# Loop order of transfers: two stores, then two loads, per pair of tiles, in an instance normalisation bound by its transfers

## Chip, cores, metric

One core of a Trainium2 chip. The metric is device time in microseconds (us), median of the executions of a run. Every run names its state; all those compared here were recorded as fast.

## The reference

```python
x: (256, 256, 4096) float32, standard normal;  eps = 1e-5
mean = np.mean(x, axis=2, keepdims=True)
var = np.var(x, axis=2, keepdims=True)
return ((x - mean) / np.sqrt(var + eps)).astype(np.float32)
```

65,536 rows of 4096 numbers are normalised one by one: 1 GiB is read and 1 GiB written.

## The kernel before

A tile is 512 rows (128 partitions x 4 rows, 8 MiB); there are 128 tiles and three buffers. The issuing queue (SyncE) starts all transfers; VectorE and ScalarE compute. VectorE's first pass takes the row sums and multiplies the tile by 1/4096 in place ("in-place means"), which the later scale undoes; ScalarE takes the sums of squares; both share the last pass. The parts that matter here:

```python
BUFS = 3; L0 = 2; rounds = (ntiles - 5) // BUFS          # 41
def store(s, t):
    take(S, done[s], K + 1)                              # wait for the compute of this tile
    S.dma_start(out=rows_of(out_t, t), in_=X[s][:, :, :]).then_inc(stored[s], 16)
def load(s, t, wait=True):
    if wait:
        take(S, stored[s], 16)                           # wait until the buffer's last store has landed
    S.dma_start(out=X[s][:, :, :], in_=rows_of(x_t, t)).then_inc(loaded[s], 16)
# VectorE, per tile (cut)
take(V, loaded[s], 16)
for r in range(4):
    V.tensor_scalar(out=x[:, r, :], in0=x[:, r, :], scalar1=1.0 / d, ..., accum_out=mean[s][:, r:r+1]).then_inc(means, 1)
...   # reciprocal, bias, then four passes x*rstd+nbias, each .then_inc(done[s], 1)
# issuing queue (cut): tile 0 in halves, then
with S.Fori(0, rounds) as i:
    for t in range(L0, L0 + BUFS):
        store(t % BUFS, (t, BUFS, rounds, i))
        load((t + 2) % BUFS, (t + 2, BUFS, rounds, i))
```

## Time and profile before

| | before |
|---|---|
| median, range | 4962.77 us, 4962.52 to 4963.97 (3 runs) |
| span of the profiled run | 4960.0 us |
| VectorE / ScalarE busy | 66% / 49% |
| DMA engines busy, rate | 100% of the span, 433 GB/s |

The prediction shows the lines that carry this.

The issuing queue in order of time (start, duration of the issue, line, what):

```profile
1003.20 0.34 SPq L165 DMA_DIRECT2D out_dram<-x  x1
1003.78 0.35 SPq L170 DMA_DIRECT2D x<-in_x_dram  x1
1042.14 0.34 SPq L165 DMA_DIRECT2D out_dram<-x  x1
1042.72 0.35 SPq L170 DMA_DIRECT2D x<-in_x_dram  x1
```

A store and the load two tiles ahead go out together, every 38.9 us here.

### The profile page before, as it was taken

How to read it: one execution, taken by the hardware profiler on the slowest of the kernel's cores; microseconds unless marked ns; L12 is line 12 of the kernel's file. 1: busy time of each engine (PE TensorE's matmuls, PEld its weight loads, DVE VectorE, ACT ScalarE, POOL GpSimd, SP SyncE). 2: the span in 40 equal slices, each digit the busy share in tenths (PEclk: the TensorE clock that was granted, in tenths of full speed). 3: DMA queues.
4: the chain of work that ended last, by engine and by line, in shares of the span. 5: the costliest groups of instructions: out<-in, count | busy, mean ns of one | idle time of the engine just before them, and what ended most of it. 6: DMA issues, size and time to landing. Idle time of an engine off the chain costs nothing.

```text
span 4960.0 us, 5954 instructions
## 1 busy us (share of the span) xinstructions
DVE 3298.0 (66%) x2049; ACT 2407.6 (49%) x1412; POOL 0.2 (0%) x4
## 2 busy tenths in 40 slices
DVE  6666666666666666666666666666666666666666
ACT  4454444554445544455445544455444554445544
POOL 0000000000000000000000000000000000000000
DMA  9999999999999999999999999999999999999999
GB/s 423 431 437 432 431 437 432 432 438 433 434 435 432 435 434 432 436 434 432 436 434 432 437 433 432 438 433 432 438 432 434 435 433 435 434 432 436 434 432 403
DMA packets 37298, 2147.52 MB, mean 433 GB/s; under 512 B 4144, under 2 KB 4144, under 8 KB 4144
## 3 DMA queue, kind: packets, MB, share of 16 engines
q1 hardware_dynamic: 37296, 2147.50, 100.0%
q14 instruction: 2, 0.02, 0.0%
HBM read 1073.74 MB, written 1073.74 MB: 433 GB/s over the span
## 4 chain that ended last, share of the span: by engine, by line
DVE 62%; another core or an unknown queue 31%; issue 4%; DMA 2%; ACT 0%; DVEq 0%; ACTq 0%; SPq 0%
DVE x L87 44%; DVE x L112 17%; DMA x<-in_x_dram 1%; DVE nbias L100 1%; DMA out_dram<-x 1%; DVE rstd L98 1%; ACT junk L137 0%; DVEq L68 0%; DVEq L225 0%; ACT L146 0%; ACT std L146 0%; DVEq L193 0%; ACTq L68 0%; ACTq L67 0%
## 5 line engine op out<-in xcount | busy, mean ns | idle before, releaser
L87 DVE TENSOR_SCALAR_CACHE_REDUCE x<-x 128x4096 f32<-128x4096 f32 x512 | 2232.3, 4416 | 1579.9 <-DMA x<-in_x_dram 1579.9
L137 ACT ACTIVATE junk<-x,mean 128x4096 f32<-128x4096 f32 x512 | 1883.1, 3678 | 2366.7 <-DVE x L87 2366.7
L112 DVE TENSOR_SCALAR x<-x,rstd,nbias 128x4096 f32<-128x4096 f32 (+1 forms) x512 | 1004.2, 2004 | 33.9 <-DVE nbias L100 29.3
L151 ACT ACTIVATE x<-x,nbias,rstd 128x3072 f32<-128x3072 f32 x130 | 383.2, 2948 | 146.2 <-DVEq L68 146.2
L137 ACT ACTIVATION_READ_ACCUMULATOR junk<-x,mean 128x1 f32 x512 | 95.5, 186 | 0.0
L146 ACT ACTIVATE std<-ss,eps_tile 128x2 f32<-128x2 f32 x256 | 75.6, 295 | 19.1
L98 DVE RECIPROCAL rstd<-std 128x2 f32<-128x2 f32 x256 | 40.7, 159 | 19.4 <-ACT std L146 19.4
L100 DVE SCALAR_TENSOR_TENSOR nbias<-mean,rstd 128x2 f32<-128x2 f32 x256 | 41.1, 161 | 8.9
L87 DVE DVE_READ_ACCUMULATOR x<-x 128x1 f32 x512 | 42.4, 83 | 0.0
L137 ACT ACT_TABLE_LOAD x1 | 1.3, 1283 | 1.2 <-DVE eps_tile L222 1.2
L146 ACT ACT_TABLE_LOAD x1 | 1.3, 1283 | 0.1
L222 DVE MEMSET eps_tile<- 128x1 f32 x1 | 0.1, 59 | 1.0 <-SPq L192 1.0
L259 POOL MEMSET const-bfloat16-1.0<- 128x1 bf16 x1 | 0.1, 103 | 0.0
L259 POOL MEMSET const-uint8-127<- 128x1 uint8 x1 | 0.1, 101 | 0.0
L259 POOL MEMSET const-float32-0.0<- 128x1 f32 x1 | 0.1, 99 | 0.2 <-issue 0.2
L259 POOL MEMSET const-float32-1.0<- 128x1 f32 x1 | 0.1, 98 | 0.0
## 6 DMA issues: line engine op xcount, KB each, us to landing
out_dram<-x SPq DMA_DIRECT2D x4, 4096.0 KB, 19.4
x<-in_x_dram SPq DMA_DIRECT2D x2, 4096.0 KB, 16.8
x<-in_x_dram SPq DMA_DIRECT2D x127, 50.3
out_dram<-x SPq DMA_DIRECT2D x126, 31.5
```

The source lines that it names most:

```text
L87: V.tensor_scalar(out=x[:, r, :], in0=x[:, r, :], scalar1=1.0 / d, scalar2=None, op0=ALU.mult, op1=ALU.add, accum_out=mean[s][:, r : r + 1 ...
L98: mine(V.reciprocal(out=rstd[s][:, c], in_=std[s][:, c]))
L100: mine(V.scalar_tensor_tensor(out=nbias[s][:, c], in0=mean[s][:, c], scalar=-1.0 / d, in1=rstd[s][:, c], op0=ALU.mult, op1=ALU.mult))
L112: V.tensor_scalar(out=x[:, r, f], in0=x[:, r, f], scalar1=rstd[s][:, c], scalar2=nbias[s][:, c], op0=ALU.mult, op1=ALU.add,).then_inc(dn, 1)
L137: mine(A.activation(out=junk, in_=x[:, r, :], func=AF.Square, bias=mean[s][:, c], scale=-float(d), accum_out=ss[s][:, c]))
L146: A.activation(out=std[s][:, c], in_=ss[s][:, c], func=AF.Sqrt, bias=eps_tile, scale=1.0 / d**3).then_inc(stds, 1)
L151: A.activation(out=x[:, last, :Q], in_=x[:, last, :Q], func=AF.Identity, bias=nbias[s][:, c], scale=rstd[s][:, c]).then_inc(dn, 1)
L222: V.memset(eps_tile, eps / d**2).then_inc(ready, 1)
L259: nc = _bacc.Bacc("TRN2", target_bir_lowering=False, num_devices=1)
```

## The change

The intent: halve the number of changes between reading and writing HBM, by sending two stores, then two loads. A load now goes into the buffer of a store that was issued just before it.

```diff
                 load(1, 1, wait=False)
+                load(2, 2, wait=False)
                 store_half(0, 0, 0)
                 store_half(0, 0, 1)
-                load(2, 2, wait=False)
                 store(1, 1)
                 take(S, stored[BUFS], 16)
                 load(0, 3)
-                with S.Fori(0, rounds) as i:
-                    for t in range(L0, L0 + BUFS):
-                        store(t % BUFS, (t, BUFS, rounds, i))
-                        load((t + 2) % BUFS, (t + 2, BUFS, rounds, i))
-                load(last % BUFS, last)
-                store((last - 2) % BUFS, last - 2)
-                store((last - 1) % BUFS, last - 1)
+                load(1, 4)
+                with S.Fori(0, 20) as i:
+                    for j in range(L0, L0 + 6, 2):
+                        for t in (j, j + 1):
+                            store(t % BUFS, (t, 6, 20, i))
+                        for t in (j + 3, j + 4):
+                            load(t % BUFS, (t, 6, 20, i))
+                for op, t in ((store, 122), (store, 123), (load, 125), (store, 124), (load, 126), (load, 127),
+                              (store, 125), (store, 126)):
+                    op(t % BUFS, t)
```

The two orders are called the old order and the pair order below. A "turn" is the place where the loads end and stores begin. The "ring" is the row of transfers that have been issued and not yet carried out; it "runs dry" when the DMA engines have nothing left to do. "Stretch", in the expectations, means packets that take longer than usual.

## The prediction

> **What bounds the kernel now.** I read the page from the top: first who is busy, then whether the transfers ever pause, then what the issuing queue waits for, and last how much work lies ahead of a transfer when it is issued. The first view is the page's busy shares with its transfer lines.
>
> ```profile
> DVE 3298.0 (66%) x2049; ACT 2407.6 (49%) x1412; POOL 0.2 (0%) x4
> ...
> DMA  9999999999999999999999999999999999999999
> ...
> DMA packets 37298, 2147.52 MB, mean 433 GB/s; under 512 B 4144, under 2 KB 4144, under 8 KB 4144
> ...
> HBM read 1073.74 MB, written 1073.74 MB: 433 GB/s over the span
> ```
>
> VectorE is idle for a third of the span and ScalarE for half; the 16 DMA engines are full in all 40 slices. The bytes are the least possible (1 GiB in, 1 GiB out), so 2147.5 MB at 433 GB/s is the whole 4960 us. The next view puts stretches of equal length side by side; the columns are the busy time of each engine, granted clock, DMA share and GB/s.
>
> ```profile
> 464.40:851.40 387.00, 257.89 (x160) 187.43 (x110) 0.00 (x0) 1.00 1.00 433
> 851.40:1238.40 387.00, 257.87 (x160) 187.45 (x110) 0.00 (x0) 1.00 1.00 434
> 2000.00:2387.00 387.00, 258.52 (x161) 188.06 (x111) 0.00 (x0) 1.00 1.00 434
> 4400.00:4787.00 387.00, 257.68 (x161) 187.45 (x110) 0.00 (x0) 1.00 1.00 434
> ```
>
> Ten tile periods of 38.7 us each fill such a stretch; the DMA share is 1.00 in every one. Nothing in the steady state waits for compute. Taking the packet records of the trace one by one gives the floor: nearly all (30,880 of 32,384) of the 64 KB packets took 2418 ns, loads and stores alike. One tile transfer is 8 such packets per DMA engine plus a 4-byte semaphore packet of 9 ns, some 19.35 us, and two of them are the 38.7 us period.
>
> Third, the waits of the issuing queue (who waited for whom, total us, times, longest), and the issues (KB each where stated, median us from issue to landing):
>
> ```profile
> SPq L68 <- DVE x L112: 4756.7, 130, 38.6
> SPq L68 <- DMA out_dram<-x: 47.7, 3, 30.7
> ...
> x<-in_x_dram SPq DMA_DIRECT2D x127, 50.3
> out_dram<-x SPq DMA_DIRECT2D x126, 31.5
> ```
>
> The issuer nearly always waits for VectorE to finish a tile, which looks like a compute bound and isn't one. A store lands 31.5 us after its issue, though it takes only 19.35: it stands 12.1 us behind work that is already queued. Those 12 us are the margin of the present order. A load, issued half a microsecond later, lands at 50.3, that is 12 + 2 x 19.3.
>
> [...]
>
> **The change, part by part.** It moves only issues and their waits on the issuing queue; the instruction listings of VectorE and ScalarE are the same but for line numbers, and so are count, size and shape of the 259 transfers.
>
> (a) Bytes: unchanged. The floor stays: per DMA engine 253 whole tile transfers x 19.35 us + 6 half ones x 9.7 = 4954 us. (The quickest spacing that the semaphore packets show is 19.319 us, as successive packets overlap a little: 4946.) To this come 2.0 us to the first packet and 1.8 us after the last (4958.2 of 4960.0).
>
> (b) Changes of direction: from about 256 to about 130. What is one worth? The packets longer than 2418 ns tell. Their excess sums to 3.5 us per DMA engine on average over the whole run, of which 1.1 us is at the first load-to-store boundary (near 39 us, packets of 3.4 to 4.0 us). The rest stands at the ends of loads that a store follows, and fades out by about 550 us; then boundary after boundary costs nothing. The engines begin in step (their semaphore packets lie 0.6 us apart in the first transfers) and are pulled apart at these boundaries: the spread is 3.3 us at the 12th transfer, 6.1 at the 48th, then 6.31 constantly up to the 204th, 8.2 near the end. So the last engine ends some 6.4 us after most others (4958.2 against 4951.8). My reading is that they get in each other's way only where many turn at once. The end is set by the slowest engine, so at the very best the change saves about 6 us (0.13%). If half the turns meant half the drift it would save 3; if the drift goes on until the engines are spread, which I find likelier since it levels off by itself, it saves almost nothing and only takes twice as long to get there. I take 1 us.
>
> (c) New waits. Let T be the landing of the first load of a pair, tile j+1. The ring then holds load j+2 (to T+19.4), store j (to 38.7), and after these come store j+1 (to 58.1), load j+3 (to 77.4), load j+4 (to 96.8). Compute takes 26.3 us a tile (from the timeline: 1015.7, first mean, to 1042.1, store issue). Store j+1 can be issued at T+26.4 and is needed at T+38.7: margin 12.3 us, what it was. Load j+3 goes into the buffer of store j, so it waits for that store to land, T+40 or so, and is needed at T+58.1: margin 17 or so. Load j+4 waits for store j+1, T+59.5, needed at T+77.4: 18. Store j+2, computed from T+26.3 to T+52.3, issued at T+60, needed at T+96.8: 37. No link is negative, so the ring never runs dry and the new direct wait of a load for the store just before costs nothing.
>
> (d) Head. Loading tile 2 ahead of the stores of tile 0 lets the ring hold work until about 60 us (2 + 3 x 19.35); the stores of tile 0 end at about 80. Store 1 is issued where before it was, at 74.5: the tightest place, some 5 us of margin. No gain either, since the ring was never dry in the head before.
>
> (e) Tail. Load 127 lands at the same distance from the end: stores 125, 126 and the two halves of 127 follow it as before. The last issue was at 4941.2, 7.3 us ahead of its turn on the slowest engine. Unchanged: 0.
>
> Sum: 4962.8 + 0 (a) - 1 (b) + 0 (c, d, e) = 4961.8.
>
> **Rivals.** *The turn of direction is costly and the change saves much.* For it: packets at the first turns are up to 1.6 us longer. Against: from about 1000 to 4000 us no packet is more than 0.3 us over, with a turn each 19.35 us; at most 6 us in all are to be had: 4956. *Two stores in a row overrun something on the way to HBM.* For it: late stores (from the 214th transfer) are 0.06 us longer on the slowest engine. Against: stores 125, 126, 127 already follow each other without a load, and come at 19.40 and 19.41 us where 19.35 is usual. At 0.06 us for each of 63 pairs, 4 us more: 4966. *The load's wait for the store just ahead makes the ring run dry.* If landing took over 15 us longer than I take it to, each pair would lose the difference; a 1 us hole in each of 63 pairs makes 5025. The margins in (c) speak against it.
>
> **Range and chances.** 4961.8, with 4957 (most of the drift saved) to 4967 (drift or late store stretch grows). Two per cent are 99 us, or 1.6 us in each of 63 pairs; nothing within reach of the order is that big on the fast side, and on the slow side only a hole in the ring that I have overlooked. Faster 0.005, same 0.98, slower 0.015.
>
> **What would show it.** DMA share 1.00 and 434 GB/s in the same stretches. VectorE's busy time stays at 3298 and its total wait for loads near 1580 us, but in some 65 waits of about 25 us in place of 126 of 12.6. Of the issuer's waits some 2000 us pass from VectorE to the stores' landing (per pair 13 + 19 = 32 us, x 62), leaving about 2750. Loads land in about 37 us after issue. The prediction is wrong if a steady stretch shows a share under 0.99, or if packets after 1000 us are not 2418 ns; step (b) is wrong if the last engine ends within 3 us of the others.

What the trace does show is the rate: 65536 B / 2418 ns = 27.1 GB/s per DMA engine, 434 for 16, with 30,880 of 32,384 packets at those 2418 ns while VectorE was busy for 66% of the span. That a changed order of issues is only a changed order of transfers, and costs nothing as long as the ring never runs dry, was the assumption; part (c) rests on it, and on margins worked out from the trace. The landings fit it (31.5 us after its issue for a store, 50.3 for the load behind it), and so do the two orders without compute, timed later (e5 4960.6 us, e6 4961.5).

## More of the kernel before

The page's rate in 40 slices of 124 us, in GB/s:

```profile
GB/s 423 431 437 432 431 437 432 432 438 433 434 435 432 435 434 432 436 434 432 436 434 432 437 433 432 438 433 432 438 432 434 435 433 435 434 432 436 434 432 403
```

The slices differ because a packet is counted whole in the slice where it starts (16 packets of 64 KB more or less are some 8 GB/s); there is no hole: between 600 and 4900 us the packet records never show fewer than 16 packets under way.

## The result

The changed kernel took 4975.77 us (median of 4 runs, 4972.83 to 4979.39) against 4962.65 (4 runs, 4961.47 to 4963.97): ratio 1.0027, 95% interval 1.0012 to 1.0041. It is 13 us slower, within 2% as forecast, but outside the stated range of 4957 to 4967. Ratios are the mean time of one kernel's fast runs over that of the other's of the same rounds, so not quite the ratio of the medians.

The views of the changed kernel that answer to those of before: the page's rate lines,

```profile
DMA  9999999999999999999999999999999999999999
GB/s 422 437 430 436 431 436 431 435 432 436 431 433 433 434 434 430 432 435 431 435 430 432 431 433 434 432 432 434 433 431 436 431 431 434 434 432 435 431 431 399
```

the same stretches (busy time of VectorE and ScalarE, clock, DMA share, GB/s),

```profile
464.40:851.40 387.00, 256.53 (x161) 186.53 (x111) 0.00 (x0) 1.00 1.00 433
851.40:1238.40 387.00, 256.00 (x159) 187.42 (x110) 0.00 (x0) 1.00 1.00 434
2000.00:2387.00 387.00, 257.00 (x161) 186.99 (x111) 0.00 (x0) 1.00 1.00 434
4400.00:4787.00 387.00, 256.82 (x161) 186.83 (x111) 0.00 (x0) 1.00 1.00 433
```

the waits, VectorE's and the issuing queue's (us in total, times, longest),

```profile
DVE x L87 <- DMA x<-in_x_dram: 1599.0, 64, 26.3
```

```profile
SPq L68 <- DVE x L112: 2869.7, 69, 44.7
SPq L68 <- DMA out_dram<-x: 1956.5, 127, 38.2
```

and the issues (median us to landing).

```profile
x<-in_x_dram SPq DMA_DIRECT2D x127, 38.5
out_dram<-x SPq DMA_DIRECT2D x126, 38.9
```

All the scheduling went as foreseen: 64 waits of some 25 us, some 1900 us of the issuer's waits handed from VectorE to the landing of stores (2000 were foreseen), loads landing after 38.5 us, DMA engines busy all the time. The share of busy time doesn't tell where 13 us went, because it is 1.00 in both kernels. The packet records of the trace do. A 64 KB packet takes 2418 ns undisturbed; counted here are those at least 60 ns over, with their excess per DMA engine (a sixteenth of the sum):

```
                       whole run              after the first 600 us
before                 142 packets, 3.0 us     32 packets,  0.3 us
after                  612 packets, 15.1 us   544 packets, 13.1 us
```

The difference after 600 us, 12.8 us, is as large as the loss. It is not waiting: between 600 and 4900 us fewer than 16 packets are under way for 0.14 us per engine only. Following each engine's packets from one to the next (which can confuse two engines that run in step, but not by much in a sum) gives where they stand: of 14.4 us of lengthening per engine between the 5th and the 250th transfer, 10.1 are in loads with a store next, 2.6 in stores with a store next, 1.3 in stores with a load next, 0.4 in loads with a load next. Before, it was 2.3 us in all, 2.0 of it in loads with a store next, and nearly all early.

At a typical bad turn near 2535 us in the changed kernel, 16 packets, all started between 2535.0 and 2536.5 us, took 2.5 to 3.6 us in place of 2.4. All engines were held up at the same moment: about ten of them in the last packet of the pair's second load, the others in the middle of that load. The first packets of the store started at 2538.3 us, after the hold-up, and took 2418 ns. At the next turn nothing of the kind happened. In the kernel before, such turns become rare after 600 us and all but end by 1050 (32 packets at least 60 ns over after 600 us, 6 after 1000): the engines then stand in fixed distances to each other (6.31 us between the first and the last from the 48th transfer or so to the 204th) and no packet from 1000 to 4000 us is more than 0.21 us over. This is called settled below. In the profiled run of the changed kernel they never settle.

### The profile page after: what moved, and what is told of

Read it like the earlier page. It is cut to its first block, busy times and chain, and to the rows that moved or that the text cites. A ratio compares the mean times of both kernels' runs of the same rounds, so it can differ in the third digit from the quotient of the medians.

```text
span 4973.5 us, 5860 instructions
## 1 busy us (share of the span) xinstructions
DVE 3292.4 (66%) x2049; ACT 2407.6 (48%) x1412; POOL 0.2 (0%) x4
## 4 chain that ended last, share of the span: by engine, by line
DMA 63%; DVE 21%; another core or an unknown queue 10%; issue 4%; SPq 0%; ACT 0%; DVEq 0%; ACTq 0%
DMA x<-in_x_dram 50%; DVE x L87 16%; DMA out_dram<-x 13%; DVE x L112 5%; DVE nbias L100 0%; SPq L165 0%; ACT junk L137 0%; DVE rstd L98 0%; SPq L170 0%; DVEq L68 0%; SPq L68 0%; ACT std L146 0%; ACT L146 0%; DVEq L193 0%
## 6 DMA issues: line engine op xcount, KB each, us to landing
x<-in_x_dram SPq DMA_DIRECT2D x127, 38.5
```

## The experiments

All start from one of the two kernels. Many give a wrong output. The check of results called most of these correct all the same, since rows of normal numbers are nearly normalised to begin with. Two limits hold for all that follows. The rounds were on different chips: the record lists chip 3 for e1 to e4 and e9 to e11, 0 for e5 to e8, 6 for e12 to e15 and 12 for e16 to e18 (for the first runs of the two kernels it lists none). The kernel before was timed in each round and has a median of 4962.6 to 4963.2 in all; the changed kernel was not timed again. And except for e1, e2, e9 to e11, e14 and e15, the recorded 95% intervals of the ratios include 1, so the argument rests on ranges of single executions that don't overlap, and on the packet records.

**First four: compute at the turn (theory C), the pairing (D), or which tiles are read and written together (A).** In the old order the turn falls in VectorE's idle time (it stands idle for 12.66 us before 1015.71, when it starts on the load that has just landed), in the pair order it doesn't (at the turn near 2535 us it is at work, from 2529.0 on). And in the old order the tile being loaded at a turn follows the one being stored; in the pair order it is two tiles further.

e1, VectorE and ScalarE on a PSUM tile in place of the tiles in SBUF, in twice as many shorter steps:

```diff
-    V.tensor_scalar(out=x[:, r, :], in0=x[:, r, :], ...)        # and so on for all large passes
+    for _ in range(2): v(V.tensor_scalar(out=jv, in0=jv, ...))  # jv, ja: halves of a PSUM tile of 4096
```

> The pair order, with VectorE and ScalarE working on PSUM alone, for about as long as before (wrong output on purpose: x is stored as it was loaded). Theory C (the packets at a load-to-store turn are stretched because VectorE and ScalarE use SBUF just then, which in the old order they never do): about 4962 us, stretched packets gone after the first 600 us, like the kernel before. Theory D (the order itself: engine phases that never settle because loads and stores come in pairs): about 4976 us, some 15 us of stretch per DMA engine. Theory A (the distance between the tile being loaded and the tile being stored at the turn, 2 in place of 1): about 4976 too.

Measured: 4988.02 us (4986.58 to 4990.21), before 4962.88. Worse than the changed kernel, with no bulk traffic in SBUF at all. C falls as I had put it.

e2, two more VectorE passes per tile in the old order:

```diff
+    for r in range(2): mine(V.tensor_scalar(out=x[:, r, :], in0=x[:, r, :], scalar1=1.0, ...)); V.wait_ge(own_v, own)
```

> The old order with two more passes of VectorE over SBUF per tile (8.8 us), so that VectorE is busy at the load-to-store turn, with 3 us of margin left in the ring. Theory C: stretched packets at the turns all through the run, time about 4970 to 4985. Theories A and D: the packets stay at 2418 ns after the first 600 us, time about 4963 to 4965.

Measured: 5085.0 us (5075.33 to 5092.32). The stretches show that here the ring did run dry:

```profile
464.40:851.40 387.00, 338.49 (x197) 183.05 (x108) 0.00 (x0) 1.00 0.99 425
2000.00:2387.00 387.00, 337.75 (x197) 187.09 (x110) 0.00 (x0) 1.00 1.00 425
```

The packet records have some 55 us of idle time per DMA engine between packets, where the kernel before has under 3. So it doesn't answer the question; it shows what a margin of 3 us is worth. The rest of the 122 us is lengthened packets, 69 us per engine: with the ring dry now and then, the engines stand lined up (all but one within 0.4 us at the 56th landing) and lose some 0.55 us per tile. Some 50 us of this stand in stores with a load next, so at the other change of direction and not at the turn that the theories are about.

e3, the pair order with even tiles in the lower half of the tensor and odd ones in the upper, so that neighbours in time at a turn are neighbours in memory again:

```diff
+    def place(t): return ntiles // 2 * (t % 2) + t // 2
-            return ap[t]
+            return ap[place(t)]
```

> The pair order with even tiles in the lower half of the tensor and odd ones in the upper, so that at a load-to-store turn the tile loaded lies one tile after the tile stored, as in the old order. Theory A: about 4962 to 4965. Theories C and D: about 4976, unchanged.

Measured: 4970.07 us (4969.83 to 4971.18): 5.7 us better than the changed kernel, not the 13 that A wanted.

e4, the old order written out (no loop), over even tiles, then odd ones, `place(t) = 2 * (t % 64) + t // 64`.

> The old order (unrolled on the issuing queue) over even tiles and then odd ones, so that at a load-to-store turn the tile loaded lies two tiles after the tile stored, as in the pair order. Theory A: about 4976. Theories C and D: about 4962.

Measured: 4968.84 us (4967.26 to 4970.6). It looked like the other half of A, and it was not: see e7.

**Next four: take the compute away; controls for the addresses.**

```diff
# e5 (old order), e6 (pair order): all compute replaced by
+    take(V, loaded[s], 16); V.sem_inc(done[s], k + 1)
# e7: old order, the loop of issues written out; e8: the same, with e3's place(t)
-    with S.Fori(0, rounds) as i: ...
+    for t in range(L0, L0 + BUFS * rounds): store(t % BUFS, t); load((t + 2) % BUFS, t + 2)
```

> The old order with no work on VectorE and ScalarE at all (wrong output on purpose); every store is issued as soon as its tile has landed, so the ring holds some 38 us of work in place of 12. If when a transfer is issued, and what stands in the ring at a turn, makes the difference between the two orders, this loses its settled state: over 4966 us and stretch at turns through the whole run. If only the order of transfers and the addresses count: 4962 to 4963, stretch gone after some 600 us.

Measured: 4960.61 us (4960.34 to 4961.61).

> The pair order with no work on VectorE and ScalarE (wrong output on purpose). If compute or the moment of issue causes the stretch: 4962 to 4966. If the pair order itself does: 4974 to 4988, with stretch at load-to-store turns up to the end.

Measured: 4961.52 us (4960.89 to 4961.84). Without compute the pair order settles like the old one (91 long packets after 600 us in place of 544) and costs the same to 1 us. D falls: neither the pairs nor half the turns cost or gain anything by themselves. The heads of the two pages, changed kernel and e6 in turn:

```profile
span 4973.5 us, 5860 instructions
```

```profile
span 4959.8 us, 1498 instructions
```

> The old order with its loop of issues written out, a control for the run with tiles two apart, which was written out too. If writing out had caused its 6 us: about 4969. If the distance of two tiles did: 4962 to 4963, as the kernel before.

Measured: 4967.31 us (4966.01 to 4968.69). So writing out the loop costs 4.7 us, and of e4's 6.0 only 1.5 are left for the distance of two tiles, with ranges that overlap. The written-out program has 6 instruction fetches beside the transfers where the kernel before has 2; whether they cause it was not tried by itself. The trace of e8, which has the same fetches, speaks against it: between 600 and 3500 us, with fetches at 699, 1933 and 3173, its lengthened packets add up to 0.08 us per engine, and its loss (5.0 us) comes after 4000. In the changed kernel all three fetches are at 103 and 4835 us, so its loss in between is not theirs.

> The old order, written out, with even tiles in the lower half of the tensor and odd ones in the upper: at a load-to-store turn the tile loaded lies half a tensor from the tile stored. If the stretch depends on the addresses read and written together, this differs from the kernel before in its settled stretch, in either direction (4958 to 4961, or over 4966). If only the time order of turns counts: 4962 to 4963.

Measured: 4968.65 us (4967.16 to 4969.2), 1.3 above its control e7. In the old order the place of the tiles makes no difference clear of the ranges. In the pair order e3 stands 5.7 us under the changed kernel, measured on different rounds; part of the loss may hang on it.

**Three on the property of compute: late issue of the stores (I) or memory traffic (M).** Without compute a tile's store is also issued 26 us earlier, so e6 changed two things (and, as came out later, a third: the number of instructions).

```diff
# e9: every instruction as in the changed kernel, on one partition
-    x[:, r, :]
+    x[0:1, r, :]
# e10: e1, but the tile is released before its compute
+    V.sem_inc(dn, k + 1)          # directly after the load has landed
# e11: e1's compute in the old order
```

> The pair order with every instruction of VectorE and ScalarE in place and as long as before, but on one partition in place of 128 (wrong output on purpose). Stores are issued as late as in the changed kernel, while the traffic of compute in SBUF is gone. Theory I (the second store of a pair is issued too late, some 12 us before its turn on the slowest engine, while the leading DMA engines are 10 us ahead): about 4974 to 4980, stretch to the end. Theory M (the memory traffic of compute stretches the packets): about 4961 to 4963, as without compute.

Measured: 4973.32 us (4969.94 to 4975.91). Of the 13 us of loss 10 are there (before: 4963.17 in these rounds) with 1/128 of the traffic: M falls as the main cause.

> The pair order with the compute on PSUM of the first experiment, but each tile released for its store as soon as it has landed, compute running beside it (wrong output on purpose). Theory I: about 4961 to 4963, settled, though VectorE and ScalarE are as busy as in the run that took 4988. Theory M: about 4980 to 4990.

Measured: 4976.51 us (4975.6 to 4977.77). Early issue wins 11 us of e1's, but it does not bring 4961 to 4963: I falls as the only cause. The loss has another form here. The last packets of twelve DMA engines end by 4959 us, one engine ends at 4972.6, alone: it has fallen behind steadily, 12.2 us between the 100th and the 250th transfer, where the second slowest lost 0.9.

> The old order with the compute on PSUM of the first experiment, about 29 us a tile where it was 26 (wrong output on purpose): a control. Theory I: the spread of the DMA engines (6 us) stays below the margin (some 9 us), so 4961 to 4966. Theory M: over 4970.

Measured: 4995.02 us (4981.89 to 5016.82). The old order loses its settled state too, under this compute (428 GB/s from 4400 to 4787 us of the profiled run, where the kernel before has 434). What e1, e10 and e11 have in common is some 9,000 to 9,500 instructions, against 5,860 in the changed kernel. That gave theory N: the number of instructions that run beside the transfers.

**Four to tell I, M and N apart.**

```diff
# e12 (one partition) and e13 (128): all compute replaced by two long VectorE passes per tile
+    for h in range(2): V.tensor_scalar(out=x3072, in0=x3072, scalar1=1.0, ..., accum_out=...)   # 4 x 3072 elements: three of the tile's four rows
# e14 (pair order) and e15 (old order): release at landing, then
+    for h in range(32 * k): V.reciprocal(out=mean[s][0:1, 0:1], in_=eps_tile[0:1]); V.wait_ge(own_v, h + 1)
```

> The pair order; in place of the compute two instructions of VectorE per tile, of some 13 us each, on one partition (wrong output on purpose), so that stores are issued as late as in the changed kernel but with few instructions and no traffic. Theory I (late issue alone): 4970 to 4976, stretch to the end. Theory N (the number of instructions that run beside the transfers keeps the DMA engines from settling): 4961 to 4963. Theory M (traffic): 4961 to 4963.

Measured: 4961.19 us (4960.73 to 4965.48).

> The same two long instructions per tile on all 128 partitions: late issue, few instructions, full traffic in SBUF (output wrong on purpose). Theory I: 4970 to 4976. Theory N: 4961 to 4963. Theory M: 4970 to 4976, well above the run on one partition.

Measured: 4961.57 us (4961.19 to 4962.27). This is the strongest single run. VectorE's line in e13, then in the changed kernel:

```profile
DVE 3318.8 (67%) x521; POOL 0.2 (0%) x4
```

```profile
DVE 3292.4 (66%) x2049; ACT 2407.6 (48%) x1412; POOL 0.2 (0%) x4
```

The issuer's wait for VectorE in e13 (the changed kernel's is shown above):

```profile
SPq L68 <- DVEq L85: 2854.2, 69, 44.7
```

VectorE is as long at work, on some five sixths of the elements, and the issuer waits for it as long (2854 us against 2870); only it does so in a quarter of the instructions, and ScalarE in none. The pair order then costs nothing. I falls, and M for VectorE's traffic; ScalarE's traffic is not in e13, but e9 lost 10 us with next to none.

> The pair order; each tile is released for its store as soon as it has landed, and VectorE then runs 128 instructions on single elements (wrong output on purpose): early issue, many instructions, no traffic. Theory N: over 4970, one DMA engine that falls behind steadily. Theories I and M: 4961 to 4963.

Measured: 5222.63 us (5221.26 to 5224.77).

> The old order with the same 128 instructions on single elements per tile and early release (wrong output on purpose). Theory N: over 4966. Theories I and M: 4960 to 4962, as without compute.

Measured: 5215.05 us (5214.65 to 5215.83). Far more than N expected, and spoilt as a test: the written-out instructions were fetched over and over. Transfer lines of e14:

```profile
DMA packets 37505, 2149.21 MB, mean 411 GB/s; under 512 B 4144, under 2 KB 4144, under 8 KB 4144
...
q14 instruction: 209, 1.71, 0.1%
```

209 fetches of 8 KB, where the changed kernel has 3. Their share of the engines' time is 0.1%, and yet the run loses 5%. In e15 the rate stays at 431 to 434 GB/s from the second to the eighth slice and is about 411 after that, though the fetches go on all the time. So it is not shown that the fetches by themselves cost the 5%. I didn't foresee any of this, and the two runs are no test of N.

**Last three.**

```diff
# e16: as e14, but 64 instructions per tile in a small loop
+    with V.Fori(0, 2 * k):
+        for n in range(8): V.reciprocal(...).then_inc(own_v, 1); V.wait_ge(own_v, n + 1)
+        V.sem_clear(own_v)
# e17: pair order, ScalarE does nothing, std set to 1; e18: VectorE does nothing, ScalarE takes loaded and gives done
```

> The pair order with early release and 64 instructions of VectorE on single elements per tile, in a small loop this time so that no instructions have to be fetched while it runs (the two runs with 128 written out fetched 8 KB some 200 times, which spoilt them as a test). Theory N (the number of instructions): over 4968. If only the fetches did the harm: 4961 to 4963.

Measured: 4977.35 us (4976.95 to 4978.23), with 2 fetches. Its page:

```profile
DVE 1234.2 (25%) x8193; POOL 0.2 (0%) x4
...
GB/s 422 433 434 430 435 433 435 432 435 432 435 433 435 432 436 432 435 433 435 432 436 432 436 432 436 432 436 432 437 432 435 433 433 433 435 432 432 433 434 369
...
q14 instruction: 2, 0.02, 0.0%
```

Stores released early, VectorE three quarters idle, each instruction touching one number; and it takes 15.8 us more than e6 (in other rounds; the kernel before took 4963.1 in these and 4962.6 in those). The last slice falls to 369 GB/s: as in e10, one engine comes home late (4973.6 us, the next at 4961.1, the median at 4957.9).

> The pair order with all the work of VectorE on all partitions and nothing on ScalarE (wrong output on purpose): late issue, full VectorE traffic, two thirds of the instructions. Theory N: 4966 to 4974, in between. If ScalarE's part alone did it: 4961 to 4963. If VectorE's part: 4973 or more.

Measured: 4965.4 us (4964.98 to 4965.73). Without ScalarE's part the factor 1/4096 of the in-place means stays in, which is meant. It lies at the lower edge of the range that N gave, a little below it.

> The pair order with the work of ScalarE alone (wrong output on purpose): some 19 us a tile, a third of the instructions. Theory N: 4961 to 4968. If ScalarE's part alone did it: 4973 or more.

Measured: 4963.15 us (4962.53 to 4964.45), as N has it. VectorE's part alone costs 2.3 us, ScalarE's 0.1, both together 13: not a plain sum.

Put together by the instructions on each page's head:

| pair order | instructions | median us | | old order | instructions | median us |
|---|---|---|---|---|---|---|
| e6 none | 1498 | 4961.5 | | e5 none | 1592 | 4960.6 |
| e12, e13 two long | 2148 | 4961.2, 4961.6 | | e7, e4, e8 written out | 5375 | 4967.3, 4968.8, 4968.7 |
| e18 ScalarE alone | 2923 | 4963.2 | | before | 5954 | 4962.7 |
| e17 VectorE alone | 3689 | 4965.4 | | e11 PSUM | 9548 | 4995.0 |
| after, e9, e3 | 5860 | 4975.8, 4973.3, 4970.1 | | | | |
| e10 PSUM, early | 9068 | 4976.5 | | | | |
| e1 PSUM | 9454 | 4988.0 | | | | |
| e16 short ones, early | 12893 | 4977.4 | | | | |

e2 (dry ring) and e14 and e15 (fetches) are left out. The old order doesn't follow the count: e7 has fewer instructions than the kernel before and takes longer. No version beats the kernel before by more than 2 us, and those that do beat it don't compute the result.

## Why the prediction was wrong, point by point

**(a) Bytes and floor: right.** The runs without compute end within 8 us of the 4954 us of packets, and settled packets took 2418 ns in both directions and both orders.

**(b) What a turn is worth: wrong.** The step that failed is "if the drift goes on until the engines are spread, which I find likelier since it levels off by itself, it saves almost nothing". In the old order it does level off; I took that for a property of the transfers; the runs point to one of transfers and instruction stream together. With the real compute, 544 packets of the pair order were lengthened after 600 us, most of them at turns, by 13.1 us per engine, up to the very end. In e6 and e13, with few instructions, the same order levels off as I said, and takes 4961 to 4962, the number that I gave. So the term of the sum that stands at -1 was +13. The sign that I had set for (b), a last engine within 3 us of the others, would have missed this: the last engine ends at 4971.6 us and most at 4965.3, as far apart as before, and all of them are 13 us later. The general sign did show it: after 1000 us, 509 packets are at least 60 ns too long. One reading was off as well: in the kernel before, lengthened packets last to 1050 us, not 550.

**(c) Waits, (d) head, (e) tail: right.** The DMA share stayed at 1.00, and the margins held; where one was taken away (e2), the ring ran dry and the loss was 122 us, 55 of them idle.

**The rivals.** None was the cause. "Two stores in a row overrun something" was nearest in size (4966), but stores with stores next have only 2.6 of the 14.4 us, and e6 and e13 have the same pairs of stores without loss.

**What is shown and what isn't.** Shown: the loss is lengthened packets, most of them at the turn; it is absent with the order alone (e6) and with VectorE as busy and the stores as late (e13), each on a chip on which the changed kernel was not timed; and a loss of the same size, if of another form, is brought on by nothing but short instructions (e16). Between 1,500 and 5,860 instructions the pair order's time rises with their number; beyond that, other things count as well (e10 and e16 issue early and lie below e1). Not separated: instructions from the semaphore updates that go with them, which rise together (5,392 updates in e13's trace, 8,083 in the changed kernel's, 14,219 in e16's). Seen but not explained: two forms of loss, the common hold-up at a turn (changed kernel, e1) and one engine that falls behind (e10, e16).

A later count on the kept traces says more on the second form. Between 2500 and 3500 us each DMA engine takes some 413 packets of 64 KB. Add up, engine by engine (followed from packet to packet as above), those that are too long by less than 60 ns: 15 engines have at most 0.3 us each, and one has more, in the pair order the more instructions run:

| | e6 | e13 | e18 | e17 | e3 | e9 | e10 | e16 | before (old order) |
|---|---|---|---|---|---|---|---|---|---|
| instructions | 1498 | 2148 | 2923 | 3689 | 5860 | 5860 | 9068 | 12893 | 5954 |
| excess of that one engine, us | 0.7 | 1.2 | 1.5 | 1.9 | 2.7 | 2.8 | 4.0 | 4.1 | 1.5 |

These runs are from all four chips. So one engine is slowed by some 2 to 10 ns per packet (0.7 to 4.1 us over 413) in every one of them. In e9 it falls from 0.1 to 4.9 us behind the second slowest between the 76th and the 176th landing, while the other form is nearly absent: 0.3 us of lengthened packets per engine from 1200 to 3200 us. After 3400 us these are back, with 4.5 us. So the pair order with all its 5,860 instructions can settle and come apart again, with the lag of one engine first. That the lag brings on the hold-ups is not tested.

Open is how an instruction reaches a DMA engine: no run or trace here shows a way. Whether the recording of the profile has a part in it can't be told either: every timed run lists a span and a granted clock from its records, so there is none without them to compare. Open too is why the pair order gives way at 5,860 instructions while the old order holds at 5,954 (its slow engine loses 1.5 us in the count above, not 2.7). That it holds only just is the reading of its own repeats, for which no packet records are kept: among the runs of the kernel before beside e12 to e18 are one of 4996.81 us and one of 4998.54, all others of those rounds lying between 4961.9 and 4963.9; beside e9 to e11 there is one of 4968.57. The first two widen the intervals of those ratios, so there the medians are compared. And whether e3's 5.7 us are an effect of addresses stays open.

## What to carry to other kernels

Here, with the DMA engines full, a different order of the same transfers had nothing to win but the few microseconds of lengthened packets, so count these first: 3 us in 4960. A turn from loads to stores cost up to 1.6 us on a packet in the kernel before at its first turn, near 39 us, next to nothing once settled (6 packets at least 60 ns over after 1000 us), and 0.2 us on average in the changed kernel, where the engines don't settle (10.1 us over some 60 turns). Judge such a kernel by the packet records, not by the busy share, which was 1.00 in the good and the bad version alike. And try a shorter instruction stream beside saturated transfers, in a loop: here as much of VectorE's time in a quarter of the instructions cost less (e13), and the two runs with 128 written-out instructions per tile, fetched again and again, lost 5%, though which of the two did it was not separated.
